# One core of Trainium2: a gated recurrence whose runs of 32 tokens are met in one product in place of six levels of products

## The chip, the cores and the metric

The program runs on one core of a Trainium2 chip. The metric is the device time of one execution in microseconds (us), the median over several runs. The engines are named as the profile names them: PE (matrix products; PEld are its weight loads), DVE (vector), ACT (scalar), POOL (GpSimd) and SP, whose queue issues the transfers.

## The reference, cut to what matters

The layer mixes 4,096 tokens (and 16 meta tokens ahead of them) in two ways: sparse attention over the 256 keys that an indexer picks for each query, and a gated linear recurrence. The change is in the recurrence, which is this for each of 4 heads of 128 features:

```python
def hgrn2(q, f_raw, i, lb):
    """f = lb + (1-lb) sigmoid(f_raw), S_t = diag(f_t) S_{t-1} + (1-f_t) i_t^T, o_t = S_t^T q_t."""
    ...
    bcum = jnp.cumsum(gc, axis=2)                     # gc = log f
    o_inter = jnp.einsum('bhtk,bhkv->bhtv', qc * jnp.exp(bcum), state)
    diff = bcum[:, :, :, None, :] - bcum[:, :, None, :, :]
    decay = jnp.exp(jnp.where(tri[:, :, None], diff, -jnp.inf))
    scores = jnp.sum(qc[:, :, :, None, :] * decay * kc[:, :, None, :, :], axis=-1)
    o_intra = jnp.einsum('bhts,bhsv->bhtv', scores, vc)
    new_state = (jnp.exp(b_last[:, :, 0, :])[..., None] * state
                 + jnp.einsum('bhsk,bhsv->bhkv', kc * jnp.exp(b_last - bcum), vc))
```

A score of query t and key s is a product over features, weighed by all gates between s and t. The lower bound `lb` is zero for a model of one layer, so a gate is a plain sigmoid.

## The kernel before, in words

The program has two regions. In the first (up to 2,100 us) four kinds of work lie side by side: the input projections of attention (`phase_a`, streams A and B), the indexer's scores (stream T, products `kidx,qi`), the search for the threshold of the 256 best keys (stream S, `topk_search`, on DVE and ACT), and the recurrence (streams P for its projections and C for the rest), first for heads 0 and 1, then for heads 2 and 3, each over 16 segments of 256 tokens. Stream P ends with 16 segments of plain projections, the gate path of the recurrence (`gh_d`). The second region is the attention and the output projection.

Work of the first region is recorded and then laid out by a planner (`Plan.run`), which walks a model of the engines and issues for each engine the ready work of the stream with the lowest number in `RANK`; the order on each engine is fixed by it before the program runs, and an engine waits where the next instruction in its order isn't ready. On PE the indexer (T, 0) goes first and the projections of the recurrence (P, 3) fill what is left. On DVE the search (S, 2.5) has the highest number, so it takes what the recurrence (C, 1.5) and the projections leave.

In `hgrn_chunks` a chunk is 128 tokens; two chunks and two heads are done together, which makes 32 passes (2 head pairs by 16 segments). The scores of a chunk are put together in `scT` by halving. A first product of keys and queries gives the diagonal. Then there are seven levels, with runs of B = 1, 2, 4, ..., 64 tokens: at each, the keys of the first half of a pair of runs meet the queries of the second half, both already multiplied by the gates up to the border between the halves. POOL makes these products with gates (`qp`, `kp`, `fp` are queries, keys and gate products of a segment), PE the scores (four products, one for each head and chunk), and DVE copies those that belong to the level into `scT` under a mask (`lmask`); at the last two levels (B of 32 and 64) the products are small and ACT copies them. POOL may multiply the queries only when the level's product has read them.

After the planner's work, `topk_unresolved` counts the queries whose threshold the search couldn't settle (`bad`) with one product and three small DVE instructions, and every engine branches on the count: over an exact search that is in the program for that case. In the profile nearly all of the first region's work shows as line L400, the planner's call, so rows are told apart by the names of the tiles.

Of the kernel before, what the change touches and what calls it, by code (L numbers as in the profile page):

```python
# [128 lines left out]
class Base:  # L129


    def __init__(self, pool, tag, shape, dtype, make, tile=None):
        self.pool, self.tag, self.dtype, self.make, self.tile = pool, tag, dtype, make, tile
        self.row = math.prod(shape[1:])
        self.seen, self.left, self.slot, self.last = [], 0, None, None
        self.part = Part(self, np.arange(math.prod(shape), dtype=np.int32).reshape(shape))
# [63 lines left out]
class Bank0:  # L200
# [5 lines left out]
    def tile(self, shape, dtype, name):  # L206
        self.n ^= 1
        return self.real.tile(shape, dtype, name=f"bank{self.n}", bufs=1)


# [35 lines left out]
class Plan:  # L246
# [144 lines left out]
    def start(self, o, now):  # L391
        o.start = now
        for b in sorted(o.bases, key=lambda b: b.turn):
# [224 lines left out]
def topk_setup(k, p):  # L618
    nc = k.nc
    k.zero2 = p.tile([128, 2], F32, name="zero2")  # L620
    nc.vector.memset(k.zero2, 0.0)
    k.iota = p.tile([128, NEXT + 1], F32, name="iota")
    nc.gpsimd.iota(k.iota, pattern=[[1, NEXT + 1]], base=0, channel_multiplier=0, allow_small_or_imprecise_dtypes=True)
    k.bad = p.tile([128, k.NB], F32, name="bad")
    nc.vector.memset(k.bad, 0.0)
    k.mask_d = [spill(k, f"mask_d{a}", [128, 2, 256 * a + 272], U8) for a in range(k.NB // 2)]
# [238 lines left out]

def topk_unresolved(k, P):
    nc, V, tc = k.nc, k.nc.vector, k.tc
    NP = k.NB // 2
    ones = P["small"].tile([128, 1], F32, name="one1")
    V.memset(ones, 1.0)  # L870
    ps = P["ps"].tile([1, k.NB], F32, name="psi")
    nc.tensor.matmul(ps, ones, k.bad, start=True, stop=True)
    n = P["small"].tile([1, NP + 1], F32, name="nbad")
    V.reduce_sum(n[:, :NP], ps.rearrange("p (a i) -> p a i", i=2), axis=mybir.AxisListType.X)
    V.reduce_sum(n[:, NP:], n[:, :NP], axis=mybir.AxisListType.X)
    ni = P["small"].tile([1, NP + 1], I32, name="nbadi")
    V.tensor_copy(ni, n)
    some = nc.values_load(ni[0:1, NP:NP + 1], min_val=0, max_val=128 * k.NB)
    with tc.If(some > 0):
        for a in range(1, NP):  # L880
            v = nc.values_load(ni[0:1, a:a + 1], min_val=0, max_val=256)
            with tc.If(v > 0):
                topk_exact(k, a, P)

# [19 lines left out]


def hgrn_setup(k, p, P):
    nc = k.nc

    k.lmask = p.tile([128, 7, 4, 64], U8, name="lmask")
    lm = P["t"].tile([128, 7, 64], F32, name="qp")  # L910
    nc.sync.dma_start(lm, k.I["lmask"])
    for c in range(4):
        nc.gpsimd.tensor_copy(k.lmask[:, :, c, :], lm)

# [18 lines left out]

def hgrn_proj(k, g, seg, x, w, P):

    nc, V = k.nc, k.nc.vector
    meta = seg < 0
# [30 lines left out]
    nc.scalar.activation(v, p, AF.Copy)  # L968
    if meta:
        return qp, kp, fp, v  # L970
# [21 lines left out]

def hgrn_chunks(k, g, seg, S, qp, kp, fp, v, P):

# [92 lines left out]
def hgrn(k, P):  # L1087
    nc = k.nc
    nseg = k.S // 256
    for g in range(2):  # L1090
# [8 lines left out]
        state = P["s"].tile([128, 2, 128], F32, name="S", bufs=4)  # L1099
        nc.vector.memset(state, 0.0)  # L1100
        for seg in range(-1, nseg):
            nc.stream = "P"
            x = load_x(k, P, seg)
            out = hgrn_proj(k, g, seg, x, w, P)
            nc.stream = "C"
            state = hgrn_chunks(k, g, seg, state, *out, P)

    nc.stream = "W"
    w = [load_weights(k, P, [(0, COLS["g_h"] + 256 * i, 256)], nc.gpsimd) for i in range(2)]
    for seg in range(nseg):  # L1110
# [16 lines left out]
        for t in range(2):  # L1127
# [5 lines left out]
            nc.vector.tensor_tensor(sg, p, sg, ALU.mult)  # L1133
            nc.sync.dma_start(k.gh_d[2 * seg + t], sg)


def region_ab(k):

    tc, nc = k.tc, k.nc
    with ExitStack() as es:  # L1140
# [31 lines left out]
        for n in ("kidx", "widx", "bad", "zero2", "iota"):  # L1172
# [643 lines left out]
def layout(inputs):  # L1816
# [15 lines left out]
    a["lmask"] = lm  # L1832
    dist = 399 - np.arange(656)
    n = np.maximum(dist, 0)
# [24 lines left out]
```

## Time and profile before

| | |
|---|---|
| median of 3 runs | 4174.2 us (4164.69 to 4175.08) |
| profiled execution | 4170.36 us, span 4168.5 us |
| first region, ends | 2099.3 us |
| PE busy, whole span | 3982.0 us (96%) |
| DVE busy, whole span | 3211.3 us (77%) |
| ACT, POOL busy | 2470.1 us (59%), 2025.6 us (49%) |

Busy time is the time in which the engine had an instruction in work; its share is an average over the two regions. The span is what the profile covers, from the first to the last instruction; the execution's own time is 1.9 us longer.

### The profile page before, as it was taken

What the parts mean: (1) busy time and instruction counts of PE and PEld (TensorE: products, weight loads), DVE (VectorE), ACT (ScalarE), POOL (GpSimd) and SP (SyncE); (2) the same over time, 40 slices, a digit from 0 to 9 for tenths busy, and PEclk for the clock granted to TensorE, in tenths of its full rate; (3) what the DMA queues carried; (4) which work ended last, traced back from release to release, by engine and by line L of the source; (5) the groups of instructions that cost most, each with busy time, mean ns of one, the idle gap of its engine ahead of it and who ended that gap; (6) DMA issues with size and microseconds to landing.
All of it is one profiled execution on the core that took longest, in us unless ns stands there. A gap on an engine that the chain in (4) does not pass through costs nothing. (4 is left out here: it accounts for less than half of the span.)

```text
span 4168.5 us, 84763 instructions
## 1 busy us (share of the span) xinstructions
PE 3982.0 (96%) x29043; PEld 3693.6 (89%) x29043; DVE 3211.3 (77%) x10335; ACT 2470.1 (59%) x4879; POOL 2025.6 (49%) x2806
## 2 busy tenths in 40 slices
PE   8999989999999999999989999999999999979998
PEld 8889989999989998999979998999899899967886
DVE  3889979888977978687158878888888888856665
ACT  4565655555466473744157777788778878851111
POOL 3322243443443424242036776778677767753222
PEclk9999989999999999999999999999999999989999
DMA  7776752222232222225651223114212311145552
GB/s 226 236 217 217 226 178 71 84 77 76 89 97 97 84 62 79 70 91 186 235 154 52 62 78 95 58 58 128 61 47 68 110 52 49 44 136 175 167 166 101
DMA packets 396601, 475.16 MB, mean 114 GB/s; under 512 B 54672, under 2 KB 276192, under 8 KB 395648
## 3 DMA queue, kind: packets, MB, share of 16 engines
q1 hardware_dynamic: 396160, 469.65, 36.4%
q8 instruction: 231, 3.78, 0.4%
q14 instruction: 210, 1.72, 0.1%
HBM read 314.51 MB, written 156.65 MB: 113 GB/s over the span
## 5 line engine op out<-in xcount | busy, mean ns | idle before, releaser
L400 PE MATMUL bank<-x,x 128*128 128x256 f32 (+2 forms) x10944 | 1486.5, 287 | 28.5 <-ACT x L400 12.0
L400 PEld LDWEIGHTS bank<-x,x 128*128 128x128 f32 (+1 forms) x10944 | 1400.5, 191 | 54.8 <-ACT x L400 12.8
L1279 PE MATMUL lg<-kt,aq 128*128 128x494 f32 (+16 forms) x2560 | 647.5, 376 | 23.9 <-ACT mn L1279 18.4
L1279 DVE CUSTOM_DVE_ANT_0 L<-lg,am,mx 128x464 f32<-128x464 f32 (+10 forms) x784 | 541.1, 692 | 105.1 <-PE lg L1279 52.8
L1279 DVE TENSOR_TENSOR tl<-pt,th 128x512 fp32r<-128x512 f32 (+1 forms) x848 | 533.0, 665 | 106.8 <-ACT th L1279 78.3
L1279 ACT ACTIVATE L<-L,mx 128x2056 f32<-128x2056 f32 (+26 forms) x384 | 569.7, 1486 | 75.6 <-DVE mx L1279 75.0
L1279 PE MATMUL pt<-ident,L 128*128 128x128 f32 x4224 | 566.6, 274 | 13.9 <-ACT raw L1279 11.4
L1279 PE MATMUL po<-th,vt 128*128 128x256 f32 (+1 forms) x2176 | 560.1, 290 | 4.7 <-POOL th L1581 3.7
L1279 PE MATMUL po<-tl,vt 128*128 128x256 f32 (+1 forms) x2176 | 540.5, 284 | 15.3 <-POOL tl L1582 12.8
L1279 ACT ACTIVATE th<-pt 128x512 fp32r<-128x512 f32 (+1 forms) x848 | 456.5, 584 | 124.1 <-PE pt L1279 108.8
L1279 PEld LDWEIGHTS pt<-ident,L 128*128 128x128 f32 x4224 | 479.3, 141 | 44.6 <-ACT raw L1279 14.4
L400 POOL TENSOR_TENSOR qp<-qp,fp 128x256 f32<-128x256 f32 (+1 forms) x256 | 213.9, 836 | 571.8 <-PE bank L400 518.8
L1279 PEld LDWEIGHTS lg<-kt,aq 128*128 128x128 f32 x2560 | 418.6, 190 | 68.3 <-DVE mx L1279 26.3
L400 ACT ACTIVATE bank<-bank 128x452 f32<-128x452 f32 (+28 forms) x600 | 305.7, 527 | 263.5 <-PE bank L400 230.6
L1279 PEld LDWEIGHTS po<-tl,vt 128*128 128x128 f32 x2176 | 413.9, 190 | 32.9 <-POOL tl L1582 21.2
L1581 POOL TENSOR_SCALAR th<-raw 128x512 fp32r<-128x512 f32 x240 | 358.4, 1493 | 169.3 <-ACT raw L1279 147.8
L400 DVE SCALAR_TENSOR_TENSOR rows<-bank,widx,rows 128x452 f32<-128x452 f32 (+28 forms) x600 | 407.2, 682 | 33.8 <-ACT bank L400 24.0
L1279 PEld LDWEIGHTS po<-th,vt 128*128 128x128 f32 x2176 | 413.1, 190 | 13.5 <-POOL th L1581 7.0
L400 ACT ACTIVATE mask<-rows,cur 128x944 uint8<-128x944 f32 (+14 forms) x320 | 381.5, 1195 | 66.1 <-DVE cur L400 61.6
L400 PE MATMUL bank<-kidx,qi 128*128 128x450 f32 (+30 forms) x1200 | 353.9, 384 | 21.1 <-DMA qi<-qi_d 11.3
L1498 POOL TENSOR_TENSOR nb<-mn,tb 128x272 f32<-128x272 f32 (+2 forms) x256 | 228.8, 897 | 256.6 <-DMA kt<-kst_d 138.9
L1582 POOL TENSOR_TENSOR tl<-raw,th 128x512 fp32r<-128x512 f32 x240 | 309.5, 1290 | 16.0
(231 smaller groups left out, 6501.7 us busy)
## 6 DMA issues: line engine op xcount, KB each, us to landing
x<-xs_d SPq DMA_DIRECT2D x384, 256.0 KB, 3.5
xs_d<-x SPq DMA_DIRECT2D x128, 256.0 KB, 2.6
aq<-qa_d SPq DMA_DIRECT2D x128, 256.0 KB, 3.9
x<-in_xT_dram SPq DMA_DIRECT2D x64, 256.0 KB, 3.7
kst_d<-kp SPq DMA_DIRECT2D x128, 128.0 KB, 2.5
vst_d<-fp SPq DMA_DIRECT2D x64, 256.0 KB, 2.6
vt<-vst_d SPq DMA_DIRECT2D x64, 256.0 KB, 4.4
x<-in_x_dram SPq DMA_DIRECT2D x32, 512.0 KB, 4.3
```

Of the source, the lines that this page charges most:

```text
L400: o.ins = getattr(eng.real, f)(*(real(x) for x in a), **{n: real(x) for n, x in kw.items()})
L1279: r = f(*args, **kw)
L1498: POOL.tensor_tensor(nb[:, :Wi - nf], pair["mn"][:, i, :Wi - nf], tb[0]["tb"][:, t0:t0 + Wi - nf], ALU.subtract)
L1581: POOL.tensor_scalar(s["th"], s["raw"], 1.0, None, ALU.mult)
L1582: POOL.tensor_tensor(s["tl"], s["raw"], f32(s["th"]), ALU.subtract)
```

## The change

In the 32 passes of `hgrn_chunks` with real tokens, the diagonal product and the five levels B = 1 to 16 are replaced. POOL still multiplies keys with gates at these levels (so that a key carries all gates from behind it to the end of its run of 32), and now the whole second half of the gate products too (so that `fp` holds at each token the gates from the start of its run). The queries are multiplied once by `fp` and then by `ri`, the inverse of the run's whole gate product, which gives `qx`. One product of `kp` and `qx` gives all scores within the runs of 32, and DVE copies them into `scT` under one mask, `tri`. `scT` is cleared once for each head pair and kept. Levels 32 and 64 stay as they were.

The inverse is held in float32 by a bound: `ri` uses the larger of the gate product and 2^-100, `hmin` keeps the smallest gate product seen, and `count_unresolved` counts the runs below the bound with the unsettled queries. If there are any, `hgrn_exact` does the whole recurrence again by the old levels, in the branch behind the region. The count is now recorded as planned work on stream S, and the branch stands alone behind the plan.

```diff
@@ hgrn_chunks
-    copy = None
-    if not meta:
+    copy, lev0 = None, 0
+    if sc is not None:
+        lev0 = int(math.log2(HB))
+        for l in range(lev0):
+            B = 1 << l
+            kv = kp.rearrange("p h (n a b) -> p (h n) a b", a=2, b=B)
+            tv = fp.rearrange("p h (n a b) -> p (h n) a b", a=2, b=B)
+            nb = 2 * 256 // (2 * B)
+            nc.gpsimd.tensor_tensor(kv[:, :, 0, :], kv[:, :, 0, :], tv[:, :, 1, B - 1:B].to_broadcast([128, nb, B]), ALU.mult)
+            nc.gpsimd.tensor_tensor(tv[:, :, 1, :], tv[:, :, 1, :], tv[:, :, 0, B - 1:B].to_broadcast([128, nb, B]), ALU.mult)
+        runs = lambda x: x.rearrange("p h (n b) -> p (h n) b", b=HB)
+        nr = 2 * 256 // HB
+        ri = P["s"].tile([128, nr, 1], F32, name="ri")
+        V.tensor_scalar(ri, runs(fp)[:, :, HB - 1:HB], HMIN, None, ALU.max)
+        V.reciprocal(ri, ri)
+        nc.gpsimd.tensor_tensor(qp, qp, fp, ALU.mult)
+        qx = P["t"].tile([128, 2, 256], F32, name="qx", bufs=1)
+        nc.gpsimd.tensor_tensor(runs(qx), runs(qp), ri.to_broadcast([128, nr, HB]), ALU.mult)
+        V.tensor_tensor(k.hmin.rearrange("p (n b) -> p n b", b=1), k.hmin.rearrange("p (n b) -> p n b", b=1),
+                        runs(fp)[:, :, HB - 1:HB], ALU.min)
+        pl = P["pl"].tile([128, 4, 128], F32, name="a")
+        for hc in range(4):
+            sl = slice(128 * (hc % 2), 128 * (hc % 2) + 128)
+            nc.tensor.matmul(pl[:, hc, :], kp[:, hc // 2, sl], qx[:, hc // 2, sl], start=True, stop=True)
+
+        def copy(pl=pl):
+            V.copy_predicated(sc, k.tri, pl)
+    elif not meta:
...
-    for l in range(nlev):
+    for l in range(lev0, nlev):
@@ hgrn
+        sc = P["t"].tile([128, 4, 128], F32, name="scT", bufs=1)
+        nc.gpsimd.memset(sc, 0.0)
...
-            state = hgrn_chunks(k, g, seg, state, *out, P)
+            state = hgrn_chunks(k, g, seg, state, *out, P, sc if seg >= 0 else None)
@@ region_ab
+        plan.stream = "S"
+        count_unresolved(k, T)
         with tc.manual_schedule():
             plan.run()
...
-        topk_unresolved(k, T)
+        unresolved(k, T, G)
@@ unresolved, behind the exact searches
+        v = nc.values_load(ni[0:1, NP:NP + 1], min_val=0, max_val=128 * 16)
+        with tc.If(v > 0), tc.manual_schedule():
+            hgrn_exact(k, P)
```

The planner lays out the whole first region anew. On POOL, in the middle of the region, one pass stood like this before (a row is line, operation, output and inputs by tile names, and the output's shape):

```order
L400 TENSOR_TENSOR qp<-qp,fp 128x512
L400 TENSOR_TENSOR qp<-qp,fp 128x256
L400 TENSOR_TENSOR kp<-kp,fp 128x256
L400 TENSOR_TENSOR fp<-fp 128x256
L400 TENSOR_TENSOR qp<-qp,fp 128x128x2
L400 TENSOR_TENSOR kp<-kp,fp 128x128x2
L400 TENSOR_TENSOR fp<-fp 128x128
L400 TENSOR_TENSOR qp<-qp,fp 128x64x4
L400 TENSOR_TENSOR kp<-kp,fp 128x64x4
L400 TENSOR_TENSOR fp<-fp 128x64
```

and stands like this in the change:

```order
L415 TENSOR_TENSOR kp<-kp,fp 128x256
L415 TENSOR_TENSOR fp<-fp 128x256
L415 TENSOR_TENSOR kp<-kp,fp 128x128x2
L415 TENSOR_TENSOR fp<-fp 128x128x2
L415 TENSOR_TENSOR kp<-kp,fp 128x64x4
L415 TENSOR_TENSOR fp<-fp 128x64x4
L415 TENSOR_TENSOR kp<-kp,fp 128x32x8
L415 TENSOR_TENSOR fp<-fp 128x32x8
L415 TENSOR_TENSOR kp<-kp,fp 128x16x16
L415 TENSOR_TENSOR fp<-fp 128x16x16
L415 TENSOR_TENSOR qp<-qp,fp 128x512
L415 TENSOR_TENSOR qx<-qp,ri 128x512
```

The multiplications of the queries, each of which waited for a product of PE, have gone from between the levels; ten instructions on keys and gates follow each other, and two on the queries come last.

On PE, in the same part of the region, a level with runs of 16 stood between indexer products (`kidx,qi`) and projections (`x,x`) before:

```order
L400 MATMUL bank_14558<-kidx,qi 128x472 x2
L400 MATMUL bank_14565<-qp,kp 128x64 x2
L400 MATMUL bank_14570<-kidx,qi 128x472 x2
L400 MATMUL bank_14565<-qp,kp 128x64 x2
L400 MATMUL bank_14447<-x_9027,x_14034 128x256
L400 MATMUL bank_14447<-x_9039,x_14034 128x256
L400 MATMUL bank_14581<-kidx,qi 128x472 x2
```

Now the one product of a pass stands there:

```order
L415 MATMUL bank_13944<-x_8819,x_13576 128x256
L415 MATMUL bank_14038<-kidx,qi 128x472 x2
L415 MATMUL bank_14042<-qx,kp 128x128 x4
L415 MATMUL bank_14051<-kidx,qi 128x472 x2
L415 MATMUL bank_13944<-x_8862,x_13576 128x256
```

The four products with 64 columns, of which a pass had five such groups, are no longer there; the four with 128 columns take the place of the diagonal's four.

On DVE, at the end of the region, the order before was this (`qp<-bank` are the last pieces of the gate path, `nbad` the count):

```order
L400 TENSOR_TENSOR qp<-bank_28830,qp 128x256
L400 TENSOR_TENSOR qp<-bank_28836,qp 128x256
L400 TENSOR_TENSOR qp<-bank_28840,qp 128x256
L874 TENSOR_REDUCE nbad<-bank_28944 1x16
L875 TENSOR_REDUCE nbad<-nbad 1x1
L877 CAST nbadi<-nbad 1x17
L878 TENSOR_LOAD nbadi
L879 COMPARE_AND_BRANCH
```

and it is this in the change:

```order
L415 SCALAR_TENSOR_TENSOR bad<-b_27775,b_27800 128x2
L415 TENSOR_REDUCE nbad<-bank_27859 1x17
L415 TENSOR_REDUCE nbad<-nbad 1x1
L415 TENSOR_TENSOR qp<-bank_27709,qp 128x256
L415 TENSOR_TENSOR qp<-bank_27717,qp 128x256
L415 TENSOR_TENSOR qp<-bank_27722,qp 128x256
L415 TENSOR_TENSOR qp<-bank_27727,qp 128x256
L415 CAST nbadi<-nbad 1x18
L415 TENSOR_TENSOR qp<-bank_27879,qp 128x256
```

The count has moved from behind the last work of the region to right behind the search's last instruction (`bad`), with the last eight pieces of the gate path after it. On PE the count's product (`bad,one`) was the last instruction of the region and now has 104 projections behind it; behind the last indexer product there were 1,872 projections and now there are 1,101. In the branch, the block that holds `hgrn_exact` has 6,627 PE instructions.

## Rows read from the trace of the kernel before

**Rows 1.** The page's first part: busy us of each engine (share) xinstructions.

```profile
PE 3982.0 (96%) x29043; PEld 3693.6 (89%) x29043; DVE 3211.3 (77%) x10335; ACT 2470.1 (59%) x4879; POOL 2025.6 (49%) x2806
```

**Rows 2.** Busy time by stretch: length, then each engine; clock, DMA share, GB/s last.

```profile
core 0: us, PE busy (x) PEld busy (x) DVE busy (x) ACT busy (x) POOL busy (x), PEclk, DMA share, GB/s
...
590.00:1930.00 1340.00, 1296.29 (x10390) 1231.59 (x10389) 1088.54 (x3838) 767.24 (x1640) 556.45 (x904) 0.99 0.27 84
1930.00:2100.00 170.00, 169.29 (x1412) 169.02 (x1410) 67.59 (x195) 23.23 (x63) 2.38 (x2) 1.00 0.66 220
2100.00:2118.00 18.00, 0.35 (x1) 0.38 (x2) 0.42 (x4) 1.28 (x2) 0.00 (x0) 0.55 0.61 190
```

**Rows 3.** PE, 590 to 1930 us, groups by shape: busy us, mean ns | idle before, releaser.

```profile
L400 PE MATMUL bank<-x,x 128*128 128x256 f32 x6272 | 869.2, 287 | 0.0
L400 PE MATMUL bank<-qp,kp 128*128 128x64 f32 x1280 | 175.5, 273 | 20.9 <-POOL kp L400 17.7 <-DVE rows L400 0.9 <-DVE scT L400 0.8
```

**Rows 4.** PE in order of time around 1275 us: start, us, instruction, count.

```profile
1273.39 1.11 PE L400 MATMUL bank<-qp,kp 128*128 128x64 f32 x8 [0.33 <-POOL kp L400]
1274.30 2.40 PE L400 MATMUL bank<-x,x 128*128 128x256 f32 x18
1276.54 1.00 PE L400 MATMUL bank<-qp,kp 128*128 128x64 f32 x8
1277.35 1.56 PE L400 MATMUL bank<-x,x 128*128 128x256 f32 x11
```

**Rows 5.** PE's waits, 590 to 1930 us: us in total, times, longest.

```profile
PE bank L400 <- POOL kp L400: 17.9, 32, 3.2
```

**Rows 6.** POOL, 590 to 1930 us, groups by shape, then by tile.

```profile
L400 POOL TENSOR_TENSOR qp<-qp,fp 128x256 f32<-128x256 f32 x224 | 171.0, 763 | 209.3 <-PE bank L400 208.7
L400 POOL TENSOR_TENSOR kp<-kp,fp 128x256 f32<-128x256 f32 x224 | 165.6, 739 | 0.0
L400 POOL TENSOR_TENSOR qp<-qp,fp 128x512 f32<-128x512 f32 x32 | 43.0, 1342 | 362.5 <-PE bank L400 310.1 <-DVE x L400 18.0 <-DVE rows L400 17.3
L400 POOL TENSOR_TENSOR fp<-fp 128x256 f32<-128x256 f32 x32 | 23.7, 740 | 2.5
...
L400 POOL TENSOR_TENSOR fp<-fp 128x4 f32<-128x4 f32 (+6 forms) x230 | 92.8, 403 | 18.0
```

**Rows 7.** The tile `kp` on POOL: duration ns min/median/max.

```profile
L400 POOL TENSOR_TENSOR kp<-kp,fp x232: 216/672/1831, 588.8 to 1915.9; 128x256 f32<-128x256 f32 x112, 128x16 f32<-128x16 f32 x4
```

**Rows 8.** DVE, 590 to 1930 us, groups by shape.

```profile
L400 DVE COPY_PREDICATED scT<-lmask,bank 128x256 f32<-128x256 uint8 x160 | 88.9, 556 | 27.3 <-PE bank L400 26.3
L400 DVE TENSOR_SCALAR cx<-cur 128x2 f32<-128x2 f32 x92 | 22.7, 247 | 1.4
L400 DVE TENSOR_TENSOR scT<-bank,ident 128x512 f32<-128x512 f32 x32 | 22.0, 687 | 7.6 <-PE bank L400 7.3
```

**Rows 9.** DVE's waits, 590 to 1930 us.

```profile
DVE cur L400 <- ACT mask L400: 99.6, 79, 6.2
```

**Rows 10.** In order of time: last indexer products, last `bad`, PE's last 327 projections.

```profile
1846.73 0.57 PE L400 MATMUL bank<-kidx,qi 128*128 128x448 f32 x2
1981.57 0.16 DVE L400 SCALAR_TENSOR_TENSOR bad<-b,b 128x2 f32<-128x2 f32 x1
2059.74 39.40 PE L400 MATMUL bank<-x,x 128*128 128x256 f32 x327
```

**Rows 11.** In order of time, all engines, from the region's end to the attention's first product.

```profile
2099.07 0.22 PE L872 MATMUL bank<-bad,one 128*1 128x32 f32 x2
...
2100.33 0.17 DVE L877 CAST nbadi<-nbad 1x17 int32<-1x17 f32 x1
2106.41 0.34 SPq L1426 DMA_DIRECT2D kt<-kst_d  x1
...
2117.65 7.06 PE L1279 MATMUL lg<-kt,aq 128*128 128x464 f32 x20 [18.36 <-ACT mn L1279]
```

More of the change, by code (lines that the diff above doesn't have):

```diff
@@ L208, in tile, with __init__ @@
         return self.real.tile(shape, dtype, name=f"bank{self.n}", bufs=1)
+class InTurn:
+    def __init__(self, real, name, which):
+        self.real, self.names, self.n = real, [f"{name}{b}" for b in which], 0
+    def tile(self, shape, dtype, name):
+        self.n += 1
+        return self.real.tile(shape, dtype, name=self.names[self.n % len(self.names)], bufs=1)
 class Kind:
@@ L392, in start @@
         o.start = now
-        for b in sorted(o.bases, key=lambda b: b.turn):
+        for b in sorted(o.bases, key=lambda b: (b.turn, b.n)):
             if b.slot is None:
@@ L863, in topk_exact, with count_unresolved, unresolved @@
         nc.sync.dma_start(k.mask_d[a][:, i], gt)
-def topk_unresolved(k, P):
-    nc, V, tc = k.nc, k.nc.vector, k.tc
+def count_unresolved(k, P):
+    nc, V = k.nc, k.nc.vector
     NP = k.NB // 2
-    ones = P["small"].tile([128, 1], F32, name="one1")
+    hb = P["small"].tile([128, 16], F32, name="hb", bufs=1)
+    V.tensor_scalar(hb, k.hmin, HMIN, None, ALU.is_lt)
+    V.reduce_sum(k.bad[:, k.NB:k.NB + 1], hb, axis=mybir.AxisListType.X)
+    ones = P["small"].tile([128, 1], F32, name="one1", bufs=1)
     V.memset(ones, 1.0)
-    ps = P["ps"].tile([1, k.NB], F32, name="psi")
+    ps = P["ps"].tile([1, k.NB + 2], F32, name="psi")
     nc.tensor.matmul(ps, ones, k.bad, start=True, stop=True)
[L873 to L878, printed above, removed]
+    n = P["small"].tile([1, NP + 2], F32, name="nbad", bufs=1)
+    V.reduce_sum(n[:, :NP + 1], ps.rearrange("p (a i) -> p a i", i=2), axis=mybir.AxisListType.X)
+    V.reduce_sum(n[:, NP + 1:], n[:, :NP + 1], axis=mybir.AxisListType.X)
+    k.nbad = P["c"].tile([1, NP + 2], I32, name="nbadi")
+    V.tensor_copy(k.nbad, n)
+def unresolved(k, T, P):
+    nc, tc, ni = k.nc, k.tc, k.nbad
+    NP = k.NB // 2
+    some = nc.values_load(ni[0:1, NP + 1:NP + 2], min_val=0, max_val=128 * (k.NB + 16))
     with tc.If(some > 0):
@@ L968, in hgrn_proj @@
     nc.scalar.activation(v, p, AF.Copy)
-    if meta:
+    if meta or not gate:
         return qp, kp, fp, v
@@ L1134, in hgrn, with hgrn_exact @@
             nc.sync.dma_start(k.gh_d[2 * seg + t], sg)
+def hgrn_exact(k, P):
+    nc = k.nc
+    nc.stream = None
+    k.lmask = P["lm"].tile([128, 7, 4, 64], U8, name="lmask")
+    lm = P["t"].tile([128, 7, 64], F32, name="qp")
+    nc.sync.dma_start(lm, k.I["lmask"])
+    for c in range(4):
+        nc.gpsimd.tensor_copy(k.lmask[:, :, c, :], lm)
+    for g in range(2):
+        w = {n: load_weights(k, P, [(0, COLS[c] + 256 * g, 256)]) for n, c in (("f", "f_h"), ("q", "q_h"), ("i", "i_h"))}
+        state = P["s"].tile([128, 2, 128], F32, name="S", bufs=4)
+        nc.vector.memset(state, 0.0)
+        for seg in range(-1, k.S // 256):
+            out = hgrn_proj(k, g, seg, load_x(k, P, seg), w, P, False)
+            state = hgrn_chunks(k, g, seg, state, *out, P)
 def region_ab(k):
@@ L1171, in region_ab @@
         k.nc = nc
-        for n in ("kidx", "widx", "bad", "zero2", "iota"):
+        for n in ("kidx", "widx", "nbad", "zero2", "iota", "lb", "lbm", "hg"):
             setattr(k, n, getattr(k, n).real())
@@ L1176, in region_ab @@
         T["ps"] = Bank0(T["ps"])
-        topk_unresolved(k, T)
+        k.xs_d = {c: x.real() for c, x in k.xs_d.items()}
+        bank, place = T["pi"], T["xs"]
+        G = dict(T, **{n: InTurn(bank, "bank", b) for n, b in (("pj", (0, 1, 2)), ("pl", (3, 4)), ("ps", (5, 6, 7)))},
+                 **{n: InTurn(place, "x", range(*b)) for n, b in (("wh", (0, 12)), ("wl", (12, 24)), ("wr", (24, 28)),
+                                                                  ("xs", (28, 44)), ("lm", (44, 45)))})
+        unresolved(k, T, G)
 def rsqrt_mean(k, pool, ss, inv, w):
@@ L1832, in layout @@
     a["lmask"] = lm
+    s, t = np.arange(128)[:, None], np.arange(128)[None, :]
+    a["tri"] = ((s // HB == t // HB) & (t >= s)).astype(np.float32)
     dist = 399 - np.arange(656)
```

23 lines of the change are left out of this document (15 added, 8 removed).

## The prediction

> **What bounds the kernel now.** I read the page first. PE is busy for 96% of the span, DVE for 77%, ACT and POOL for less [rows 1]. A share over the whole span says little, so next comes the view by stretches. The recurrence runs from about 590 to 1,930 us. There PE is busy for 1,296.3 of 1,340 us, with 43.7 us idle, DVE for 1,088.5 (81%) and POOL for 556.5 (42%), and the granted clock is 0.99, that is 2.4 GHz nearly throughout. From 1,930 to 2,100 us PE is busy for 169.3 of 170 us and DVE for 67.6 [rows 2]. So the first region ends with PE working off projections that wait for nobody, and whatever PE is spared earlier should bring these forward.
>
> The other candidate is the search. Its last instruction, `bad`, starts at 1,981.57 us, and the last indexer product at 1,846.73 [rows 10]; PE ends at 2,099.3 [rows 11]. The search is done 118 us before PE is. That is the slack in which PE's gain can be taken before something else sets the end.
>
> The trace's matmul rows need care. A group's mean of 273 ns is the time of one row with its tail, and rows overlap. What PE pays is the distance from a group's start to the next group's start: eight rows of a level take 0.91 us at 1,273.39 and 0.81 us at 1,276.54 [rows 4], so 1.72 us for 16, or 108 ns for a row. A projection costs 39.40 us / 327 = 120.5 ns [rows 10].
>
> The Trainium skill, Perfetto Trace Analysis, section Identifying the Most-Contended Engine, has it that busy matmul time is a poor measure and that the busy share of the weight loads is the better one. By that, PE has more air in the recurrence than the matmul row says: 1,231.6 of 1,340 us, 92% [rows 2]. If PE weren't full there, another engine would set the pace, and the case would be the second rival below; in the last 170 us both measures agree (169.0 and 169.3 us), so the end itself is PE's by either.
>
> **The change part by part.**
>
> *Products of the levels.* Five levels of four float32 products leave each of 32 passes: 640 products. The trace shows two rows for each, and they are the 1,280 rows with 64 columns [rows 3]. At 108 ns a row that is 138 us of PE. The bounds are 101 ns (0.81 us / 8 [rows 4]), so 129 us, and the group's busy time as a whole, 175.5 us [rows 3], which counts overlap twice. I take 138, since the start-to-start distance is what the next instruction feels. The diagonal's four products become the run's four, of the same shape: nothing.
>
> *PE's waits.* PE stood idle for 20.9 us before those rows, 17.7 of them for `kp` from POOL [rows 3], in all 32 stalls of 0.56 us on average, the longest 3.2 [rows 5]. They go, and one new wait for each pass takes their place: the one product needs everything that POOL does at the levels, then `qp` times `fp`, then `qx`. The bounds of that wait are nothing and, with the longest stall in each pass, 32 x 3.2 = 102 us. I take 0.5 us for each, near the mean stall, 16 us: the net is -5 us. It is this small because of what covers POOL. The ten instructions on keys and gates need only the gate projection; behind it PE still has 144 projections of the same segment (queries, values, gate path: 48 each), 144 x 0.1205 = 17.4 us. The chain costs 5 x 0.739 + 5 x 0.740 = 7.4 us, and the two on the queries 2 x 1.342 = 2.7 us [rows 6]. Only these 2.7 us stand behind the queries' projection, and the values and the gate path (96 projections, 11.6 us) are still there to cover them. If that cover were gone, a pass would show all 10.1 us; that is the first rival.
>
> *POOL.* A pass now costs 7 x 0.763 + 7 x 0.739 + 1.342 us and 92.8 / 32 = 2.9 us for `fp`, 14.8 us. After: 2 x 0.763 + 7 x 0.739 + 5 x 0.740 + 2 x 0.403 + 2 x 1.342 = 13.9 us [rows 6]. Over 32 passes POOL has 28 us less, at 42% load: nothing on the path. It also no longer waits for a level's product before it may change the queries.
>
> *DVE.* A pass loses five masked copies of 0.556 us and the diagonal's 0.687 us, 3.47 us. It gains a masked copy of 512 elements, which no row shows: between 0.556 us (256 elements) and twice that; I take the middle, 0.83 us. And it gains three instructions on 16 elements, bounded by nothing and by 0.247 us, the row of two elements with the longest mean [rows 8]; at 0.247 they are 0.74 us. Net 1.9 us, 61 us over 32 passes. It isn't on PE's path, but the search takes what is left of DVE, so this decides how far the search comes forward.
>
> *The search and the count.* In the changed order 1,101 projections stand behind the last indexer product, where 1,872 did: PE's order assumes that the search does not come forward as far as the rest. By the sum below PE would end at about 1,955 us; the count's product stands 104 projections (12.5 us) before that, at 1,942. It waits for `bad`, which now must start 40 us earlier than 1,981.57 or PE stops there, with the 104 projections queued behind it and the attention behind those. DVE's 61 us are more than 40, if the search was held up by DVE. I take no stall, and price it below.
>
> *The branch.* Between the count's last instruction at 2,100.33 us and SP's first transfer for the attention at 2,106.41 lie 5.9 us, and PE's first product starts at 2,117.65 [rows 11]. The count's chain of 1.4 us (2,099.07 to 2,100.50) leaves the path, since the number is there before the region ends. What of the 5.9 us is the load of the number and what the jump, no row tells: the gain is between 1.4 and 7.3 us. I take 2. The clock of 0.55 in this gap [rows 2] stays, as the gap does.
>
> *The rest.* Two clearings of `scT`, and the new masks at the start, lie on POOL and SP: nothing.
>
> **The sum.** 138 + 5 + 2 = 145 us. The profiled execution took 4,170.4 us, its span and 1.9 us around it; that is 0.1% below the median of 4,174.2, inside the spread of the three runs. 4,170.4 - 145 = 4,025 us.
>
> **The rivals.**
>
> *POOL's chain holds PE (slower).* Place: the one product of each pass. PE loses where the new wait exceeds (138 + 21) / 32 = 5.0 us for a pass. For it: twelve instructions in a row on one engine, and a `kp` instruction took 1.83 us at worst where the median is 0.67 [rows 7]; twelve at 1.83 us are 22 us, above the 17.4 of cover and the 5.0 together if the two on the queries are as slow. With 10.1 us in each pass uncovered, the time would be 4,170 - 161 + 323 = 4,332 us; at 6 us it would be 4,201. Against it: the mean of `kp` is 0.739 us, the longest PE stall on POOL so far 3.2 us, and the cover. The Trainium skill, SBUF — State Buffer, section Who interferes with whom, says that a vector instruction with two inputs from SBUF and a GpSimd instruction that reads SBUF exclude each other for a whole instruction; by that each link could be held for one DVE instruction. The spread of `kp` fits that rule, and the mean shows that it is rare.
>
> *The search holds the end (a smaller gain).* If `bad` doesn't come forward at all, PE stops at the count and ends at 1,982 + 12.5 = 1,994 us in place of 2,099: 105 us and 2 for the branch, 4,063 us. For it: `cur` waited 99.6 us for ACT's counts [rows 9], a chain that the change leaves alone. Against: DVE's queue of the search shares with the recurrence, which loses 61 us.
>
> *The gates fall under the bound (the change does its work twice).* Then `hgrn_exact` runs, with 6,627 PE instructions; at 108 ns for each that is over 700 us, so 4,740 us. Against it: with `lb` zero and projections of unit spread a gate is about 0.45 in the geometric mean, 32 of them about 2^-37, far from 2^-100.
>
> *Nothing to be measured.* The new waits eat the products: 4.5 to 5.5 us for each pass, as above.
>
> **How the numbers follow.** PE's account, 4,025 us, from 3,995 (most of the 43.7 us of idle time goes too) to 4,050: 0.72. The search holds part or all of it, 4,050 to 4,070: 0.15. Waits beyond that which still leave a gain: 0.06. No change: 0.02. POOL's chain: 0.04. The branch: 0.01. A difference of about 0.3%, 12 us, is what a measurement of this kernel tells from no change. Faster 0.93, same 0.02, slower 0.05. The range from 3,998 to 4,068 leaves out the last four cases and a little on the fast side.
>
> **What would show it.** In the changed profile: the rows with 64 columns gone and PE's records fewer by 1,280; the first region's end near 1,955 us with PE at 97% or more from 590 us on; PE's waits for `qx` near 16 us in all, and none over 3 us; DVE's masked copies of 512 elements near 0.83 us; `bad` before the count's product could start; the gap at the branch shorter by 1 to 7 us. Waits for `qx` of 5 us in each pass, or a PE stop of 20 us or more at `bad`, would make the prediction wrong.

## The result and the profile after

The changed kernel takes 4,029.9 us (median of 4 runs, 4,025.7 to 4,037.8), the one before 4,169.8 us in the same comparison (4 runs): a ratio of 0.9667 with a 95% interval of 0.9645 to 0.9688. The forecast was 4,025 us. The profiled execution took 4,030.9 us with a span of 4,029.1, so 139.4 us went from the span of 4,168.5. One execution of experiment 5 (20,181 us) and one of the kernel before beside it (6,473 us) are left out of the medians and ratios below.

The first part of the page, to be read beside [rows 1]:

```profile
PE 3834.3 (95%) x27763; PEld 3553.9 (88%) x27763; DVE 3162.2 (78%) x10274; ACT 2472.4 (61%) x4879; POOL 1983.6 (49%) x2680
```

PE has 1,280 records fewer. DVE lost 49 us of busy time and POOL 42. To see where PE's time went, the view by stretches is taken from the start to the region's end, first of the kernel before (the columns are length, then PE, PEld, DVE, ACT and POOL, then clock, DMA share and GB/s), then of the change:

```profile
0.00:2099.30 2099.30, 2007.39 (x15731) 1916.73 (x15731) 1620.65 (x5947) 1128.10 (x2526) 751.13 (x1236) 0.98 0.43 134
```

```profile
590.00:1800.00 1210.00, 1153.27 (x9198) 1097.27 (x9198) 1004.42 (x3611) 711.69 (x1554) 515.56 (x770) 0.98 0.31 96
1800.00:1964.70 164.70, 164.66 (x1320) 162.78 (x1318) 105.04 (x371) 80.26 (x148) 2.70 (x4) 1.00 0.62 205
1964.70:1980.20 15.50, 0.00 (x0) 0.00 (x0) 0.84 (x3) 1.56 (x4) 0.50 (x2) 0.66 0.65 229
...
0.00:1964.70 1964.70, 1858.43 (x14451) 1775.47 (x14451) 1572.13 (x5888) 1129.84 (x2525) 710.83 (x1108) 0.98 0.46 143
```

PE's busy time fell by 2,007.39 - 1,858.43 = 149.0 us, and its idle time rose from 91.9 to 106.3 us, by 14.4. So the region ends 134.6 us earlier, at 1,964.7 in place of 2,099.3 us. The gap to the attention's first product fell from 18.4 us [rows 11] to 15.6 us, by 2.8, and the rest of the span from 2,050.9 to 2,048.9 us, by 2.0: together 139.4. As before, PE works without a pause at the end (164.66 of 164.70 us), so what it was spared earlier arrives there.

PE's groups by shape from 590 us on (busy us, mean ns | idle before, releaser), beside [rows 3]:

```profile
L415 PE MATMUL bank<-qx,kp 128*128 128x128 f32 x256 | 42.3, 304 | 14.1 <-POOL qx L415 9.7 <-DVE sg L415 4.0
L415 PE MATMUL bank<-qp,kp 128*64 128x64 f32 x256 | 22.3, 231 | 3.0 <-POOL kp L415 2.3 <-DVE rows L415 0.8
...
L415 PE MATMUL bank<-qp,kp 128*32 128x32 f32 x512 | 16.1, 199 | 22.5 <-POOL qp L415 16.2 <-DVE ri L415 4.7 <-DVE rows L415 1.4
```

The 20.9 us of idle time before the five levels are gone, and 14.1 us stand before the run's product, close to the 16 that were forecast. But 22.5 us stand before the products of level 32 (`qp,kp` with 32 columns), which waited for 0.3 us in the kernel before. In all 32 passes PE's order has that level ahead of the run's product; it needs only `qp` times `fp`, the last link but one of POOL's chain, so it is there that PE meets the chain first.

The worst place, PE in order of time (start, us, instruction, count, idle before and releaser), the stretches around it, and then three short stretches between the two stalls:

```profile
1152.93 0.45 PE L415 MATMUL bank<-qp,kp 128*32 128x32 f32 x16 [4.27 <-POOL qp L415]
1153.31 3.44 PE L415 MATMUL bank<-x,x 128*128 128x256 f32 x17
1160.75 2.04 PE L415 MATMUL bank<-qx,kp 128*128 128x128 f32 x8 [4.00 <-DVE sg L415]
```

```profile
1150.00:1160.00 10.00, 3.82 (x33) 3.68 (x33) 8.92 (x32) 4.36 (x9) 7.06 (x7) 0.69 0.00 0
1160.00:1170.00 10.00, 9.25 (x46) 9.14 (x47) 3.03 (x5) 7.77 (x17) 5.22 (x8) 0.50 0.09 30
1170.00:1180.00 10.00, 10.00 (x39) 7.47 (x38) 6.61 (x22) 4.92 (x15) 5.96 (x6) 0.50 0.42 138
1180.00:1190.00 10.00, 10.00 (x64) 8.39 (x63) 6.44 (x39) 9.05 (x21) 2.45 (x7) 0.78 0.51 155
1190.00:1200.00 10.00, 10.00 (x76) 9.38 (x75) 6.52 (x38) 7.34 (x17) 2.14 (x7) 1.00 0.64 207
```

```profile
1152.00:1153.00 1.00, 0.07 (x4) 0.07 (x6) 1.00 (x3) 0.47 (x1) 1.00 (x2) 1.00 0.00 0
1153.00:1155.00 2.00, 2.00 (x26) 1.96 (x26) 1.97 (x12) 0.00 (x0) 1.15 (x2) 0.69 0.00 0
1155.00:1157.00 2.00, 1.75 (x9) 1.65 (x8) 2.00 (x9) 0.00 (x0) 1.92 (x3) 0.50 0.00 0
```

There were two stalls of 4 us within 12 us. The granted clock was 1.00 when the first of them ended and 0.50, the level of 1.2 GHz, before the second began; it stayed there until past 1,180 us: 39 rows ran from 1,170 to 1,180 us where 76 did at the full clock from 1,190 on.

DVE, by shape, beside [rows 8]:

```profile
L415 DVE COPY_PREDICATED scT<-tri,bank 128x512 f32<-128x512 uint8 x32 | 23.3, 729 | 7.8 <-PE bank L415 7.6
L415 DVE TENSOR_TENSOR hmin<-hmin,fp 128x16 f32<-128x16 f32 x32 | 18.9, 591 | 0.0
L415 DVE TENSOR_SCALAR ri<-fp 128x16 f32<-128x16 f32 x32 | 9.7, 304 | 12.8 <-POOL fp L415 12.6
L415 DVE RECIPROCAL ri<-ri 128x16 f32<-128x16 f32 x32 | 7.7, 239 | 0.0
```

The masked copy of 512 elements took 0.73 us (forecast 0.83); the three small instructions took 1.13 us for a pass, where 0.74 was held to be the most. With the 110.9 us that left [rows 8], DVE's net is 51 us, not 61.

The region's end, in order of time, DVE and PE:

```profile
1950.45 0.15 DVE L415 SCALAR_TENSOR_TENSOR bad<-b,b 128x2 f32<-128x2 f32 x1
...
1951.77 0.22 PE L415 MATMUL bank<-bad,one 128*1 128x34 f32 x2
...
1951.93 12.74 PE L415 MATMUL bank<-x,x 128*128 128x256 f32 x104
```

The search's last instruction is 31.1 us earlier than before [rows 10]. PE's order reached the count 1.3 us after it, without a stop.

### The profile page after: what moved, and what is told of

Read it like the earlier page. It is cut to its first block, busy times and chain, and to the rows that moved or that the text cites. A ratio compares the mean times of both kernels' runs of the same rounds, so it can differ in the third digit from the quotient of the medians.

```text
span 4029.1 us, 81634 instructions
## 1 busy us (share of the span) xinstructions
PE 3834.3 (95%) x27763; PEld 3553.9 (88%) x27763; DVE 3162.2 (78%) x10274; ACT 2472.4 (61%) x4879; POOL 1983.6 (49%) x2680
## 5 line engine op out<-in xcount | busy, mean ns | idle before, releaser
L415 PE MATMUL bank<-x,x 128*128 128x256 f32 (+2 forms) x10944 | 1460.8, 287 | 25.7 <-ACT x L415 11.6
L1369 PE MATMUL lg<-kt,aq 128*128 128x494 f32 (+16 forms) x2560 | 646.9, 375 | 20.0 <-DMA kt<-kst_d 15.6
L1369 DVE CUSTOM_DVE_ANT_0 L<-lg,am,mx 128x464 f32<-128x464 f32 (+10 forms) x784 | 541.0, 692 | 106.3 <-PE lg L1369 54.0
L415 ACT ACTIVATE mask<-rows,cur 128x944 uint8<-128x944 f32 (+14 forms) x320 | 381.1, 1193 | 60.4 <-DVE cur L415 51.4
L415 POOL TENSOR_TENSOR kp<-kp,fp 128x256 f32<-128x256 f32 (+1 forms) x232 | 173.3, 747 | 417.2 <-ACT kp L415 372.7
```

Of the source, the lines that this page charges most:

```text
L1369: r = f(*args, **kw)
```

## The experiments

All are edits of the changed kernel. The added work doesn't alter the output, and no experiment leaves out a part of the reference's computation. "Last indexer" is the start of the last `kidx,qi` product, "PE's work done" the end of the region's last projection, "stop" PE's idle time before the count; these come from the profiled execution.

| kernel | median us | ratio to before [95%] | last indexer | `bad` | PE's work done | stop |
|---|---|---|---|---|---|---|
| the change | 4029.9 | 0.9667 [0.9645, 0.9688] | 1831.6 | 1950.5 | 1964.7 | 0 |
| 1: products back | 4189.9 | 1.0045 [1.0031, 1.0059] | 1832.3 | 1983.5 | 2120.1 | 0 |
| 2: copies back | 4084.7 | 0.9790 [0.9774, 0.9807] | 1907.1 | 2018.3 | 1967.1 | 51.4 |
| 3: 12 multiplications on POOL | 4181.6 | 1.0025 [1.0015, 1.0034] | 1892.9 | 2029.3 | 2113.6 | 0 |
| 4: dearer POOL in the plan | 4043.2 | 0.9695 [0.9679, 0.9711] | 1819.1 | 1936.0 | 1973.2 | 0 |
| 5: runs of 64 | 4012.0 | 0.9616 [0.9595, 0.9637] | 1821.0 | 1938.5 | 1929.4 | 9.3 |
| 6: count behind the plan | 4030.5 | 0.9666 [0.9645, 0.9687] | 1832.3 | 1951.1 | 1965.0 | 0.2 |
| 7: copies back, search first | 4089.4 | 0.9810 [0.9792, 0.9827] | 1872.3 | 1990.8 | 2021.4 | 0.2 |
| 8: 16 clearings on POOL | 4104.4 | 0.9850 [0.9828, 0.9872] | 1925.9 | 2036.7 | 1985.5 | 51.4 |
| 9: runs of 64, less DVE | 4003.3 | 0.9596 [0.9580, 0.9611] | 1814.8 | 1935.2 | 1931.8 | 3.6 |
| 10: as 8, indexer first on POOL | 4079.4 | 0.9785 [0.9770, 0.9801] | 1892.5 | 2006.9 | 1971.2 | 35.9 |

**1. PE's products alone are put back**, on operands that are at hand and into a bank that nobody reads.

```diff
         def copy(pl=pl):
             V.copy_predicated(sc, k.tri, pl)
+        for l in range(lev0):
+            px = P["pl"].tile([128, 4, 64], F32, name="a")
+            for hc in range(4):
+                c, o = hc % 2, 128 * (hc // 2)
+                nc.tensor.matmul(px[:, hc, :], v[:, c, o:o + 128], v[:, c, o:o + 64], start=True, stop=True)
```

> The changed kernel with 20 float32 products of 64 columns put back in each pass, on the values, into a bank that nobody reads; no copy by DVE and no wait on POOL comes back with them. PE's account: 640 products cost their start-to-start distance, 138 us at 108 ns a row and up to 149 at 117, so 4,030 + 138 to 149 = 4,168 to 4,179 us, ratio to the kernel before 0.998 to 1.003. Rival, the gain comes from DVE's relief and the search: the time stays at 4,030 to 4,050, ratio below 0.972.

From the start to the region's end, the columns as above:

```profile
0.00:2120.10 2120.10, 2014.20 (x15731) 1937.80 (x15731) 1574.61 (x5888) 1127.29 (x2525) 704.32 (x1108) 0.97 0.42 133
```

PE's busy time rose by 155.8 us and the region's end moved by 155.4 us: the whole gain is given back, though POOL and DVE keep what they were spared. The time is above both expectations, and 20 us above the kernel before: PE is idle for 105.9 us here up to the region's end, as in the change, where the kernel before has 91.9, and its busy time is 6.8 us longer than there. The 1,280 rows are worth 149 us by what left and 156 by what came back, 116 to 122 ns for a row, near the 120.5 ns of a projection; the forecast's 108 came from one pair of groups.

**2. DVE's work alone is put back**: the five masked copies and the pass over 512 elements, into `qx`, which has been read by then.

```diff
         def copy(pl=pl):
             V.copy_predicated(sc, k.tri, pl)
+            scr = qx.rearrange("p h (c t) -> p (h c) t", c=2)
+            V.tensor_tensor(scr, pl, k.ident.rearrange("p (o c) -> p o c", o=1).to_broadcast([128, 4, 128]), ALU.mult)
+            for l in range(lev0):
+                V.copy_predicated(scr[:, :, :64], k.tri[:, :, :64], pl[:, :, :64])
```

> The changed kernel with DVE's five masked copies of 256 elements and the pass over 512 put back in each pass, into the tile qx after it was read; PE's work is that of the change. DVE gets 32 x 3.5 = 111 us back. PE's account alone: 4,030 us, ratio 0.967, since PE's work is unchanged and the projections of the gate path fill its queue. Rival, the search stands right behind PE (its last instruction started 1.3 us before PE came to the count): the search ends up to 60 us later, PE stops at the count with 104 projections behind it, and the time is 4,050 to 4,090, ratio 0.971 to 0.981.

PE, in order of time:

```profile
2018.46 0.27 PE L415 MATMUL bank<-bad,one 128*1 128x34 f32 x2 [51.36 <-DVE bad L415]
```

The six instructions took DVE 93 us here, where those that left had taken 111. PE's own work was done at 1,967.1 us, 2.4 us later than in the change, and then it stood for 51 us until the search was through. So the gain has two conditions: PE's products must go, and DVE must be relieved, or the search, which stands right behind, takes more than a third of the gain back. The last indexer product came 75 us later too; how much of the search's delay goes through it, this run doesn't tell.

**3. POOL's chain is made longer** by twelve multiplications of 256 elements by one in each pass.

```diff
+        for _ in range(12):
+            nc.gpsimd.tensor_tensor(tv[:, :, 1, :], tv[:, :, 1, :], k.one3.to_broadcast([128, nb, B]), ALU.mult)
         runs = lambda x: x.rearrange("p h (n b) -> p (h n) b", b=HB)
```

> The changed kernel with 12 more multiplications by one of 256 elements on POOL in each pass, in the chain ahead of the queries: 12 x 0.70 = 8.4 us more in a chain of 10 us, against a cover of 17.4 us by 144 projections. If the cover holds: no more than 20 us slower, 4,030 to 4,050. Rival, PE waits for the chain as it stands: 32 x 8.4 = 269 us, so about 4,300. Between them: the stalls for qx and qp grow from 31 us to what the chain sticks out.

PE's waits from 590 us to the region's end (us in total, times, longest), then two groups of DVE, and the same two in the change:

```profile
PE bank L415 <- DVE rows L415: 82.7, 41, 37.9
PE bank L415 <- POOL qx L415: 32.8, 20, 5.8
PE bank L415 <- POOL qp L415: 11.1, 9, 3.8
```

```profile
L415 DVE SCALAR_TENSOR_TENSOR ro<-ro,ry,hgg 128x128 f32<-128x128 f32 x128 | 71.9, 619 | 0.5
L415 DVE SCALAR_TENSOR_TENSOR rz<-rz,rm 128x4 f32<-128x4 f32 x96 | 30.2, 315 | 1.3
```

```profile
L415 DVE SCALAR_TENSOR_TENSOR ro<-ro,ry,hgg 128x128 f32<-128x128 f32 x128 | 44.9, 413 | 0.9 <-DVE ry L415 0.6
L415 DVE SCALAR_TENSOR_TENSOR rz<-rz,rm 128x4 f32<-128x4 f32 x96 | 16.5, 172 | 1.0
```

The time rose by 152 us, past the kernel before, but hardly by the way that the rival named. With 12 x 0.64 = 7.6 us more in each pass, PE's waits for POOL rose only from 29 to 47 us: most of the cover held, helped by the time that PE lost elsewhere. What grew is the wait for DVE's `rows`, the indexer's sums (4.1 us in the change, 82.7 here), one of them 37.9 us long. DVE's instructions themselves became longer, and from 590 us to the region's end DVE was busy for 98 us more with nearly as many instructions (3,974 for 3,981).

```profile
1283.04 1.74 POOL L415 MEMSET mask<- 128x16 uint8 x1 [62.54 <-DVE b L415]
1285.94 1.13 PE L415 MATMUL bank<-kidx,qi 128*128 128x456 f32 x2 [37.88 <-DVE rows L415]
```

The longest wait shows how DVE's delay reaches PE: POOL stood idle, DVE worked through the end of a search, and only behind that, in the fixed orders, came POOL's next fill of `rows` and DVE's next sums. Of the 149 us by which the region's end moved, 105 are idle time of PE (79 of them for `rows`); the other 44 are longer busy time of the same 14,451 rows, at a mean granted clock of 0.95 in place of 0.98.

**4. The planner is told that POOL is slower** (2.65 in place of 2.104 ns for an element), so that it puts the products that need the chain later in PE's order.

```diff
-        ... else 36 + 2.104 * n
+        ... else 36 + 2.65 * n
```

> The changed kernel with the planner's price for a POOL multiplication raised from 36 + 2.104 ns for each element to 36 + 2.65, so 714 ns for 256 elements, where the rows show 698 to 766 and the planner assumed 575. If PE's 31 us of waits for qp, qx and ri come from products placed too early: these waits fall below 15 us and the time by 10 to 20 us, to 4,010 to 4,020. Rival, the waits are the chain's own: they stay near 30 us and the time at 4,030.

PE's longest waits, the same view:

```profile
PE bank L415 <- DVE rows L415: 35.1, 12, 14.1
PE bank L415 <- POOL qx L415: 15.6, 9, 3.7
```

The waits for `qp` went, those for `qx` rose to 15.6 us, and 35 us of waits for `rows` came in their place. It took 13 us more than the change, so neither expectation was met. The waits are a property of the whole plan; here a price nearer to the rows moved them and didn't remove them.

**5. Runs of 64 tokens**: level 32 leaves as well, and the bound is 2^-120.

```diff
-HB = 32
+HB = 64
-HMIN = 2.0 ** -100
+HMIN = 2.0 ** -120
```

> The changed kernel with runs of 64 tokens in place of 32 (the bound on the gate product lowered to 2^-120): the level of 32 with its 16 small products and two copies by ACT leaves each pass as well. PE's account: 512 rows at 29 ns, 15 us, and the 16.8 us of waits for qp that stood ahead of them; if PE alone decides, 4,000 to 4,015 us. Rival, the search stands 1.3 us behind PE already: it moves by little, PE stops at the count, and the time is 4,020 to 4,030.

```profile
1938.74 0.27 PE L415 MATMUL bank<-bad,one 128*1 128x34 f32 x2 [9.31 <-DVE bad L415]
```

This row of PE, in order of time, is the stop. PE's work was done 35.3 us earlier than in the change, and the time fell by only 17.9 us: `bad` came just 12 us earlier, and PE stood for it. So the time lies in the first expectation's range, but PE stopped as the rival said. The second region also happened to take 4.7 us more than in the change's profile, where nothing differs; that much belongs to chance.

**6. The count goes back behind the plan**, where the kernel before has it.

```diff
-        plan.stream = "S"
-        count_unresolved(k, T)
         with tc.manual_schedule():
             plan.run()
...
+        count_unresolved(k, T)
```

> The changed kernel with the count of unsettled queries and small gate products back behind the planned work, as before the change. If the count's place gives only the shorter gap: the idle time ahead of the attention's first product goes from 15.6 back to about 18.4 us, the region's end stays within 5 us of 1,964.7, and the time is 4,030 to 4,036. Rival, the place of the count in PE's order costs something that moves back: the region's end comes earlier and the time falls below 4,025.

The gap to the attention's first product is 16.5 us in place of 15.6 (two executions, one profile). The count's place is worth about 1 us, and the rest of the 2.8 us isn't its doing.

**7. As 2, with the search ahead of the recurrence on DVE.**

```diff
-            DVE=dict(A=0.5, B=-1, P=-0.5, C=1.5, W=1.5, S=2.5, T=2.5),
+            DVE=dict(A=0.5, B=-1, P=-0.5, C=1.5, W=1.5, S=1.2, T=2.5),
```

> The kernel with DVE's copies put back (4,085 us, of which PE stood 51.4 us at the count), with the search ranked ahead of the recurrence on DVE (1.2 in place of 2.5). If the stop comes from the search having only what the recurrence leaves: the search's last instruction comes at or before 1,960, the stop is below 10 us, and the time is 4,030 to 4,050. Rival, DVE's work as such is too much for the shorter region: the stop only moves, into waits of PE on the recurrence, and the time stays at 4,075 to 4,100.

PE's longest waits, the same view:

```profile
PE bank L415 <- DVE rows L415: 25.1, 9, 9.9
PE bank L415 <- DVE sg L415: 16.8, 10, 3.1
```

The stop of 51 us is gone, and PE's work was done 54 us later than in 2: from 590 us on it stood idle for 94.6 us where 2 has 58.2, and its busy time is 18 us longer at a granted clock of 0.97 in place of 0.98. The order moves DVE's lack of time from the end into the middle; it doesn't make any.

**8. POOL's chain is made longer without a read from SBUF**: sixteen clearings of `qx` (8.6 us by their mean of 0.54 us) ahead of the two multiplications of the queries.

```diff
+        qx = P["t"].tile([128, 2, 256], F32, name="qx", bufs=1)
+        for _ in range(16):
+            nc.gpsimd.memset(qx, 0.0)
         nc.gpsimd.tensor_tensor(qp, qp, fp, ALU.mult)
-        qx = P["t"].tile([128, 2, 256], F32, name="qx", bufs=1)
```

> The changed kernel with 16 clearings of qx on POOL in each pass, 16 x 0.54 = 8.7 us, about the time that the 12 multiplications took, by instructions that read nothing from SBUF. The 12 multiplications made DVE's busy time from 590 us to the region's end 98 us longer, at the same number of instructions. If DVE is held by POOL's reads (Trainium skill, SBUF — State Buffer, Who interferes with whom): DVE stays within 20 us of the change's 1,109 us, and the time at 4,030 to 4,080. Rival, any work of POOL holds DVE: DVE 1,180 us or more, and the time at 4,130 to 4,190.

The same two groups of DVE as in 3:

```profile
L415 DVE SCALAR_TENSOR_TENSOR ro<-ro,ry,hgg 128x128 f32<-128x128 f32 x128 | 47.9, 434 | 0.5
L415 DVE SCALAR_TENSOR_TENSOR rz<-rz,rm 128x4 f32<-128x4 f32 x96 | 27.0, 282 | 1.2
```

The long instruction stays near the change's 413 ns (434, where the multiplications made it 619; the runs without added work on POOL have 360 to 452). The short one looks stretched nearly as much as there, but not by the clearings. DVE and then POOL, in order of time:

```profile
736.28 0.58 DVE L415 SCALAR_TENSOR_TENSOR rz<-rz,rm 128x4 f32<-128x4 f32 x1
737.83 0.14 DVE L415 SCALAR_TENSOR_TENSOR rz<-rz,rm 128x4 f32<-128x4 f32 x1
```

```profile
736.19 0.65 POOL L415 TENSOR_TENSOR fp<-fp 128x256 f32<-128x256 f32 x1
736.78 3.45 POOL L415 MEMSET qx<- 128x512 f32 x6
```

The first `rz` fell beside a multiplication, the second beside clearings. So it is throughout: all 24 `rz` that took 0.38 us or more fell beside a multiplication of POOL's (in the change only 3 of 96 did so), and the 12 that fell beside clearings alone took 0.13 to 0.35 us. As a whole DVE's busy time up to `bad` rose by some 20 us, in place of some 90. The clearings stand behind `ri` in the chain and the multiplications of 3 ahead of it, so the two runs differ in more than the reads. The time was 4,104 us, above the first expectation and below the rival's: the last indexer product came 94 us later than in the change and the search with it, and PE stopped for 51 us.

**9. Runs of 64 with two small instructions fewer on DVE**: ACT keeps the runs' gate products, which are compared with the bound once at the count. What is left out is the larger-of ahead of the inverse; below the bound the exact branch replaces the result in any case.

```diff
-        V.tensor_scalar(ri, runs(fp)[:, :, HB - 1:HB], HMIN, None, ALU.max)
-        V.reciprocal(ri, ri)
+        V.reciprocal(ri, runs(fp)[:, :, HB - 1:HB])
...
-        V.tensor_tensor(hm, hm,
-                        runs(fp)[:, :, HB - 1:HB], ALU.min)
+        nc.scalar.activation(k.hmin[:, nr * (16 * g + seg):][:, :nr].rearrange("p (n b) -> p n b", b=1),
+                             runs(fp)[:, :, HB - 1:HB], AF.Copy)
```

> Runs of 64 as in the experiment before it, but two of DVE's three small instructions of each pass leave DVE: ACT keeps the runs' gate products (they are compared with the bound once, at the count), and the inverse is taken without the larger-of. That frees DVE of 32 x (610 + 325) ns = 30 us by the rows of the run with 64 tokens. Theory one: with runs of 64 it is DVE's load that makes the search late, and PE stops for it (9.3 us there); then bad comes 10 us earlier or more, the stop at the count falls under 2 us, and the time is 4,000 to 4,006 us. Theory two: the search's end is set by its own chain with ACT (cur waits for mask) and by PE's indexer products, and DVE's spare time isn't taken: bad stays within 4 us of 1,938.5, the stop stays, and the time is 4,009 to 4,016 us.

```profile
1935.38 0.22 PE L415 MATMUL bank<-bad,one 128*1 128x34 f32 x2 [3.55 <-DVE one L415]
```

It is the fastest of all, 167 us under the kernel before. The stop fell to 3.6 us (the row names `one`, a clearing right behind `bad`), in part because PE itself came 2.4 us later. `bad` moved only 3.4 us for the 30 us that left DVE: neither expectation is met as a whole. Of the 9 us to 5, 3.7 lie in the first region and 4.6 in the second, where the two are alike, so the profile vouches for some 4 us.

**10. As 8, with the indexer's work planned first on POOL.**

```diff
-            POOL=dict(C=-0.5, A=2, X=-0.5, W=2.5, P=0, T=2.5, S=1.5),
+            POOL=dict(C=-0.5, A=2, X=-0.5, W=2.5, P=0, T=-1, S=1.5),
```

> The 16 clearings on POOL in each pass stay, but POOL's order is planned with the indexer's work ahead of the recurrence (the order number of stream T on POOL is -1 in place of 2.5). Theory one: the clearings made the search late because the indexer's first fill of its rows stood behind them in POOL's order, so that the last indexer products moved from 1,831.6 to 1,925.9 us; then these come back to 1,870 us or earlier, PE's stop at the count falls under 20 us, and the time is 4,060 us or less. Theory two: POOL's fuller queue makes the recurrence late and that holds the rest, wherever the indexer's fill stands: the last indexer products stay later than 1,910 us, and the time stays at 4,090 to 4,120 us.

The last indexer product came back by 33 of the 94 us, `bad` by 30, and the stop fell from 51 to 36 us, between the two theories. So the indexer's place in POOL's order is about a third of what the clearings cost it; the rest is open.

## Why the prediction was right, step by step

**What bounds the kernel** was right. Experiment 1 shows it without another engine's help: PE's time came back one for one, and the weight loads' busy time rose by 162 us with it. That PEld was busy for only 92% of the recurrence [rows 2] didn't mean that another engine set the pace there.

**The products** were the right term, mis-sized: 138 us forecast, 149 to 156 measured (the 156 at a mean clock of 0.97, the change at 0.98), inside the bounds of 129 to 175. Two groups of a chosen moment [rows 4] gave 108 ns; the projections' 120.5 ns from 327 rows [rows 10] would have given 154.

**PE's waits** is the step that failed. A net of -5 us was forecast, and PE's idle time in the region rose by 14.4. Not because the run's product waited longer than thought (14.1 us for 16), but because "one new wait for each pass" was wrong: level 32 needs the same chain, stands ahead of the run's product in every pass, and waited 22.5 us by itself. For `qx` itself PE waited 9.7 us, 2.0 at the longest; for `qp` 16.8, 4.3 at the longest. From 590 us to the region's end PE is busy for 1,317.9 of 1,374.7 us, 96%, where 97% was named. Experiment 4 shows that these waits can't be priced one by one, since a plan without the one has another. What the fall of the clock behind such stalls costs in all is open; the kernel before has such falls too (a mean of 0.90 from 1,200 to 1,300 us). In experiment 3 the same rows took 44 us more of PE's time at 0.95 in place of 0.98. The products brought 11 us more than forecast and the waits took 19 us more, so 134.6 us were measured at the region's end where 143 were forecast; the branch and the second region then gave 2.8 us more than forecast. That the time came out within 5 us of the forecast is partly luck.

**POOL.** Less work was forecast, 28 us, and 42 went; the first rival was right that PE meets the chain, though first at level 32 and not at the run's product, and its price was not. (Twelve links of 1.83 us are 22.0 us, just under the 22.4 of cover and 5.0 together, not above them.) In the change PE waits for POOL for 29 us in all, far under 5 us for a pass, and experiment 3 shows most of 7.6 us more covered. A longer chain of multiplications does make the kernel slower than before, but by PE's waits for DVE's `rows` and its lower clock more than by waits for POOL.

**DVE and the search.** DVE's relief was 51 us, not 61, since three small instructions held to cost 0.74 us at most took 1.13. `bad` came 31 us earlier where 40 were asked for, and PE didn't stop only because its own work ended 10 us later than forecast. Had PE reached the count at 1,942 us, as the text has it, it would have stood for some 8 us. In experiment 5, whose work on PE ends at 1,929 us, it stands for 9.3. So the second rival was nearer than its chance of 0.15 said, and experiments 2 and 7 show that DVE's relief is a condition of the gain: without it, by either order, 55 to 60 us of it are lost. The prediction didn't look at the link between the search and the indexer. In the change and in experiments 2 and 4 to 10, `bad` follows the last indexer product by 111 to 120 us; when 7 and 10 brought that product forward, by 35 and 33 us, `bad` came 27 and 30 us earlier (in 7 the search itself was ranked ahead, too). But the indexer's end alone doesn't set it: in experiment 1 that product stands where it does in the change, and `bad` follows by 151 us, in 3 by 136 and in the kernel before by 135. What sets the search's end is open.

**The branch** was 2 us forecast and 2.8 measured, though the count's place gives only about 1 of it. The second region's 2.0 us were not forecast; it took between 2,047.8 and 2,053.6 us in experiments that don't touch it, so they may be chance. The exact branch didn't run: behind the gap follows the attention.

## What to carry to other kernels

Where a planner fills PE with work that waits for nobody, price removed products by the mean over many rows of the filling work, and expect the waits to move to the next consumer of the same chain, not to vanish with the product that showed them. Before such a gain is booked, look at what stands right behind the bound engine (here the search on DVE), and find how far that comes forward by the same edit: its new end caps what can be had. Here, with `bad` at 1,950.5 us and 13 us of projections behind the count, the cap was some 136 us by estimate, and PE gave 134.6. So a relief of an engine that isn't the bound can be a condition of a change.

## What the runs showed of the hardware

A small DVE instruction that begins beside a multiplication on POOL can last until the multiplication ends. POOL and then DVE of the change, in order of time:

```profile
1150.38 1.27 POOL L415 TENSOR_TENSOR x<-x,x 128x512 fp32r<-128x512 f32 x1
1151.62 1.26 POOL L415 TENSOR_TENSOR qp<-qp,fp 128x512 f32<-128x512 f32 x1
```

```profile
1150.48 1.19 DVE L415 TENSOR_TENSOR d<-opp,cur 128x2 f32<-128x2 f32 x1
1151.60 0.15 DVE L415 TENSOR_TENSOR q<-opp,cur 128x2 f32<-128x2 f32 x1
1151.67 1.23 DVE L415 TENSOR_TENSOR u<-opp 128x2 f32<-128x2 f32 x1
```

Three instructions on two elements: the two that began while POOL was multiplying took 1.2 us, and each ends within 0.03 us of POOL's instruction; the one that began between POOL's two took 0.15. Where an instruction falls decides its mean: in the change 12 of 32 `hmin` fell beside `qp` times `fp` and took 1.26 to 1.29 us, the others 0.17 to 0.23, which makes the 591 ns; in experiment 3, with more multiplications, the mean was 218. The Trainium skill, SBUF — State Buffer, section Who interferes with whom, has such instructions with two inputs from SBUF held for a whole GpSimd instruction that reads SBUF, and not for one that only writes. These rows, the `rz` of experiment 8 and experiments 3 and 8 as wholes agree; `hmin`, which took 0.17 to 0.49 us beside the clearings, agrees only roughly. The prediction had used the rule for POOL's links alone; its price is paid by DVE.

Instructions with one input are held as well. A copy of two elements, 5 us later, beside a multiplication of 1.26 us that began at 1,156.73:

```profile
1156.78 1.24 DVE L415 COPY hyp<-st 128x2 f32<-128x2 f32 x1
```

After a stall of 4.3 us PE's granted clock fell from 1.00 to 0.69 and then 0.50 while PE was at work again (1,152 to 1,157 us); a second stall of 4.0 us followed, and the clock stayed there until past 1,180 us. So a wait can cost more than its own length: eight rows of the run's product took 2.04 us there, where 1.16 are usual (as at 1,035 us, right behind a wait of 2.0 us).
